# The S5 layer's input matrices in a hybrid diffusion step: computed by broadcast products in the layout they are stored in, instead of by TensorE transposes

## The chip, the cores and the metric

One core of one Trainium2 chip runs the whole program once. The metric is the device time of one execution in microseconds. Three runs of the kernel before took 3233.06, 3233.39 and 3234.0 us; their median, 3233.39 us, is the time before.

## What is computed

The reference is one inference step of a four-layer backbone on 640 tokens (512 latent, 128 context) of width 1024: attention, an S5 layer, attention, attention, each followed by a gated convolutional FFN of width 2816. Only layer 1, the S5 layer, concerns this change. It has 64 groups of 16 channels, and each group has a 64-dimensional complex diagonal state per direction:

```python
a_re, a_im, bb_re, bb_im = s5_discretize(lam_re, lam_im, log_dt, b_re, b_im)
br = jnp.einsum('bsgc,gpc->bsgp', ug, bb_re)
bi = jnp.einsum('bsgc,gpc->bsgp', ug, bb_im)
hr, hi = complex_scan(a_re, a_im, br, bi, reverse)
y_dir = jnp.einsum('bsgp,gcp->bsgc', hr, c_re) - jnp.einsum('bsgp,gcp->bsgc', hi, c_im)
```

The kernel does not scan token by token. It takes eight tokens at a time: for a chunk, the state gains the sum over the eight tokens of a^k * B * u, with k from 7 down to 0 (0 up to 7 in the backward direction). The matrix of a^k * B for one group, with token and channel (8 x 16 = 128) on the rows and the state (64) on the columns, once for the real and once for the imaginary part, is the group's **input matrix**, W. It depends on weights alone.

## The kernel before, in words

All activations are float32 and each dense product is three float32r matmuls (high x high, high x low, low x high; `mm3`, L295 to L299). A weight tile takes this way (`weights`, L317): its load goes into a `raw` tile (pool of 3, L266), ScalarE rounds it to `wh` (L302), VectorE takes the rest as `wl` (L306); `wh` and `wl` have 2 buffers each. TensorE reads `wh` and `wl`, and the `raw` tile is free again when both parts are made.

The order: layer 0's attention, its output projection (`project_out`, L1068), layer 0's FFN (`ffn`, L688, from about 365 to 895 us in the trace), then layer 1, the S5 layer (`s5`, L1348), and so on. Work for the S5 layer that needs only weights is put beside the layer before it, as a list of small pieces, `todo`, from which `side(n)` (L679) takes n pieces at fixed points. The tile framework then orders each engine's instructions by the order of the text and by when it reckons them ready, allots pool buffers, and places the waits; every engine and the SP queue, which issues nearly all DMAs, work strictly in that written order.

**Parameters** (`s5_params`, L1119) run beside layer 0's output projection, in seven pieces. VectorE computes a and the factor of B for 64 rows x 128 (`four`, L1160), TensorE transposes them (L1181), VectorE forms the powers a^0 to a^8 (`pw`, L1183 to L1193, by `cmul`, L1103, all with one scratch tile `tmp`), GpSimd copies the powers into `par` in two orders, 36 copies for the output matrices (L1206) and 32 for the input matrices (L1211), VectorE forms B (`bb`, L1237), and one DMA writes `par` to DRAM as `d_par` (L1241). The initial state is loaded and transposed last (L1244 to L1251).

**Matrices** (`s5_matrices`, L1253) run in FFN 0: 16 steps (8 blocks of 4 state pairs x 2 directions), each of four pieces, mixed with 8 pieces that load a modulation weight into a `raw` tile (L1728). `up(m)` (L736) calls `side` twice, mostly for two pieces. In a step, the first piece loads `s5par` from `d_par` (L1265), forms the output matrices P on VectorE (real) and GpSimd (imaginary), three products of 128x576 on each (L1278 to L1280), and stores them (L1283); ScalarE fills `bz` (L1292). The second does 8 small matmuls for the lags (L1299). The third copies those out (L1305 to L1312) and forms Q, the input matrices with the state on the partitions, three operations of 128x512 on each of VectorE and GpSimd (L1320 to L1322), into the buffer that P had. The fourth has TensorE transpose Q in 8 pieces of 128x128 (L1328), ScalarE copy the result out of PSUM into W in `scr` by four copies of 128x256 (L1331), and SP store W to `d_w1` (L1334). P and Q share one buffer per part, `s5par` has one buffer, and W is one place in `scr`.

Of the kernel before, what the change touches and what calls it, by code (L numbers as in the profile page):

```python
# [252 lines left out]
class Kernel:  # L253
# [865 lines left out]
    def s5_params(self, sp):  # L1119
# [4 lines left out]
        self.d_par = self.dram.tile([16, 128, 392], F32, name="d_par")  # L1124
# [64 lines left out]
        tmp = sp.tile([128, 1024], F32, name="tmp")  # L1189
        for lo in (1, 2, 4):  # L1190
# [6 lines left out]
        par = sp.tile([128, 16, 392], F32, name="par")  # L1197
        for d in range(2):
            blks = slice(8 * d, 8 * d + 8)
            xs = slice(32 * d, 32 * d + 32)  # L1200
            for r in range(2):
                for q in range(9):
                    k = q if d == 0 else 8 - q
                    src = pw[:, k, r, xs].rearrange("p (b g) -> p b g", g=4)
                    o = r * 36 + q * 4
                    nc.gpsimd.tensor_copy(out=par[:, blks, o:o + 4], in_=src)  # L1206
                for q in range(8):
                    k = 7 - q if d == 0 else q
                    src = pw[:, k, r, xs].rearrange("p (b g) -> p b g", g=4)
                    o = 72 + r * 32 + q * 4  # L1210
                    nc.gpsimd.tensor_copy(out=par[:, blks, o:o + 4], in_=src)  # L1211
        yield

        for r, n in enumerate(("re", "im")):
# [3 lines left out]
            for b4 in range(4):  # L1218
# [4 lines left out]
                for t in range(2):  # L1223
                    pv = p[0:64, :].rearrange("p (b g t c) -> p t b g c", b=4, g=4, t=2)[:, t]
                    self.copy(par[t * 64:(t + 1) * 64, 4 * b4:4 * b4 + 4, 136 + r * 64:200 + r * 64]
                              .rearrange("p b (g c) -> p b g c", c=16), pv)
            yield

# [9 lines left out]
        for r in range(2):  # L1238
            nc.gpsimd.tensor_copy(out=par[:, :, 264 + r * 64:328 + r * 64],
                                  in_=bb[:, r].rearrange("p (b g) c -> p b (g c)", g=4))  # L1240
        nc.sync.dma_start(out=self.d_par.rearrange("b p x -> p b x"), in_=par)  # L1241
        yield

        st = self.raw()  # L1244
        nc.sync.dma_start(out=st[:, 0:128], in_=i["state_l1"][0].rearrange("d r (g t) p -> (d r g) (t p)", t=2))
        p = self.bankB()
        nc.tensor.transpose(out=p[:, 0:128], in_=st[:, 0:128], identity=self.ident)
        self.s0 = self.const.tile([128, 2, 2, 32], F32, name="s0")
        for r in range(2):
            v.tensor_scalar(out=self.s0[:, r], in0=p[:, 0:128].rearrange("p (d r g) -> p r d g", d=2, r=2)[:, r],  # L1250
                            scalar1=-1.0 if r else 1.0, scalar2=None, op0=ALU.mult)  # L1251

    def s5_matrices(self, pool):  # L1253

        nc = self.nc
        st = {}

        def step(blk, d):
            if (blk, d) == (0, 0):
# [4 lines left out]
            pr = pool.tile([128, 392], F32, tag="s5par", name="s5par")  # L1264
# [3 lines left out]
            w1p = [pr[:, 72 + r * 32:104 + r * 32].rearrange("p (q g) -> p g q", g=4).unsqueeze(3)  # L1268
                   .to_broadcast([128, 4, 8, 16]) for r in range(2)]
            ct = [pr[:, 136 + r * 64:200 + r * 64].rearrange("p (g c) -> p g c", c=16) for r in range(2)]  # L1270
            bb = [pr[:, 264 + r * 64:328 + r * 64].rearrange("p (g c) -> p g c", c=16) for r in range(2)]
# [41 lines left out]

            W = scr[:, 0:1024].rearrange("p (q n) -> p q n", q=8)
# [8 lines left out]
            yield  # L1323
            for h in range(2):
                p = self.bankB()
                for g in range(2):
                    for r in range(2):
# [468 lines left out]
```

## Time and profile before

| | |
|---|---|
| median of three runs | 3233.39 us |
| the profiled execution: its own time | 3232.56 us |
| its span, first to last instruction | 3230.7 us |
| mean granted TensorE clock, as a share of full speed | 0.986 |
| busy share: TensorE / weight load / VectorE / ScalarE / GpSimd | 97% / 91% / 67% / 44% / 17% |
| DMA moved | 364.30 MB, mean 113 GB/s |
| chain that ended last, by engine | TensorE 79%, VectorE 12%, ScalarE 4%, DMA 3% |

How to read it: the own time holds some 1.9 us around the span. Busy shares are means over very different stages; TensorE's busy time counts a matmul from start to modelled end, and matmuls overlap, so what one costs is read from the distance between starts. The chain is followed back from the last instruction to what released it. Line numbers are those of the code above; L302 and L306 are helpers, told apart by their tiles. "issue" as a releaser is time in which the engine waited for nothing that the profile shows.

### The profile page before, as it was taken

What the parts mean: (1) busy time and instruction counts of PE and PEld (TensorE: products, weight loads), DVE (VectorE), ACT (ScalarE), POOL (GpSimd) and SP (SyncE); (2) the same over time, 40 slices, a digit from 0 to 9 for tenths busy, and PEclk for the clock granted to TensorE, in tenths of its full rate; (3) what the DMA queues carried; (4) which work ended last, traced back from release to release, by engine and by line L of the source; (5) the groups of instructions that cost most, each with busy time, mean ns of one, the idle gap of its engine ahead of it and who ended that gap; (6) DMA issues with size and microseconds to landing.
All of it is one profiled execution on the core that took longest, in us unless ns stands there. A gap on an engine that the chain in (4) does not pass through costs nothing.

```text
span 3230.7 us, 55544 instructions
## 1 busy us (share of the span) xinstructions
PE 3120.2 (97%) x22620; PEld 2933.3 (91%) x22620; DVE 2157.9 (67%) x4070; ACT 1410.7 (44%) x2497; POOL 534.1 (17%) x916
## 2 busy tenths in 40 slices
PE   7999999989978999999999999999999999999999
PEld 6867999989966999999999889999998878999999
DVE  6666886797677368867766658677656775644543
ACT  4466443343442343433443655343344574533432
POOL 1332332353210000000013520000001431000000
PEclk8999999999998999999999999999999999999999
DMA  6251554444465324544431023344424212223221
GB/s 247 88 191 49 143 169 142 126 118 111 147 257 186 107 72 139 155 118 131 131 115 60 27 72 87 116 121 120 115 84 152 73 40 73 64 82 87 63 86 46
DMA packets 384287, 364.30 MB, mean 113 GB/s; under 512 B 39144, under 2 KB 357488, under 8 KB 374432
## 3 DMA queue, kind: packets, MB, share of 16 engines
q1 hardware_dynamic: 382752, 356.55, 35.5%
q0 software_dynamic: 1280, 4.20, 0.4%
q8 instruction: 178, 2.92, 0.4%
q14 instruction: 77, 0.63, 0.1%
HBM read 328.07 MB, written 36.83 MB: 113 GB/s over the span
## 4 chain that ended last, share of the span: by engine, by line
PE 79%; DVE 12%; ACT 4%; DMA 3%; issue 2%; POOL 1%; SPq 0%; DVEq 0%; ACTq 0%; POOLq 0%
PE psa L297 16%; PE psa L299 16%; PE psa L298 16%; PE psb L297 6%; PE psb L299 6%; PE psb L298 6%; PE psb L176 3%; PE psb L206 2%; DVE wl L306 2%; PE psb L440 1%; PE psa L110 1%; PE psa L111 1%; ACT wh L302 1%; DVE Pt L1470 1%; DVE t L715 1%
## 5 line engine op out<-in xcount | busy, mean ns | idle before, releaser
L297 PE MATMUL psa<-yh,wh 128*128 128x384 f32 (+1 forms) x2752 | 854.3, 310 | 2.6 <-ACT hb L705 1.8
L299 PE MATMUL psa<-yh,wl 128*128 128x384 f32 (+1 forms) x2752 | 850.0, 309 | 0.0
L298 PE MATMUL psa<-yl,wh 128*128 128x384 f32 (+1 forms) x2752 | 849.7, 309 | 0.3 <-POOL yl L232 0.3
L306 DVE TENSOR_TENSOR wl<-raw,wh 128x2048 fp32r<-128x2048 f32 (+2 forms) x192 | 408.9, 2130 | 269.8 <-ACT wh L302 266.1
L297 PEld LDWEIGHTS psa<-yh,wh 128*128 128x128 f32 x2752 | 521.6, 190 | 18.8 <-issue 10.3
L302 ACT ACTIVATE wh<-raw 128x2048 fp32r<-128x2048 f32 (+2 forms) x192 | 333.1, 1735 | 465.9 <-PE psa L298 428.8
L298 PEld LDWEIGHTS psa<-yl,wh 128*128 128x128 f32 x2752 | 522.1, 190 | 0.5 <-POOL yl L232 0.5
L299 PEld LDWEIGHTS psa<-yh,wl 128*128 128x128 f32 x2752 | 521.7, 190 | 0.0
L297 PE MATMUL psa<-ah,wh 128*128 128x384 f32 (+1 forms) x1184 | 366.7, 310 | 7.3 <-DVE X L663 7.3
L299 PE MATMUL psa<-ah,wl 128*128 128x384 f32 (+1 forms) x1184 | 365.7, 309 | 0.0
L298 PE MATMUL psa<-al,wh 128*128 128x384 f32 (+1 forms) x1184 | 365.5, 309 | 0.0
L663 DVE SCALAR_TENSOR_TENSOR X<-psa,modt,X 128x256 f32<-128x256 f32 x372 | 141.5, 433 | 218.7 <-PE psa L299 218.7
L306 POOL TENSOR_TENSOR yl<-scr,yh 128x256 fp32r<-128x256 f32 (+1 forms) x36 | 41.3, 1150 | 1273.5 <-ACT yh L302 1247.5
L297 PEld LDWEIGHTS psa<-ah,wh 128*128 128x128 f32 x1184 | 224.2, 189 | 12.7 <-issue 7.3
L297 PE MATMUL psb<-wh,yh 128*128 128x256 f32 x800 | 227.7, 286 | 2.6 <-ACT yh L602 2.5
L299 PE MATMUL psb<-wh,yl 128*128 128x256 f32 x800 | 226.4, 286 | 3.9 <-DVE yl L603 1.9
L298 PE MATMUL psb<-wl,yh 128*128 128x256 f32 x800 | 226.2, 285 | 0.3 <-DVE wl L306 0.3
L298 PEld LDWEIGHTS psa<-al,wh 128*128 128x128 f32 x1184 | 224.3, 189 | 0.0
L299 PEld LDWEIGHTS psa<-ah,wl 128*128 128x128 f32 x1184 | 224.1, 189 | 0.0
L497 DVE SCALAR_TENSOR_TENSOR acc<-raw,cond,acc 128x512 f32<-128x512 f32 x280 | 197.1, 745 | 33.2 <-DMA raw<-in_w_mod_dram 33.2
L715 DVE SCALAR_TENSOR_TENSOR t<-hb,cols,t 128x641 f32<-128x641 f32 x176 | 170.5, 970 | 57.6 <-ACT t L713 57.6
L705 ACT ACTIVATE hb<-psa,cols 128x512 f32<-128x512 f32 x320 | 149.9, 519 | 124.3 <-PE psa L299 124.2
(327 smaller groups left out, 6253.0 us busy)
## 6 DMA issues: line engine op xcount, KB each, us to landing
raw<-in_w_up_dram SPq DMA_DIRECT2D x176, 512.0 KB, 5.2
raw<-in_w_mod_dram SPq DMA_DIRECT2D x80, 512.0 KB, 3.9
raw<-in_w_mod_dram SPq DMA_DIRECT2D x35, 1024.0 KB, 5.1
raw<-in_w_down_dram SPq DMA_DIRECT2D x48, 640.0 KB, 3.9
raw<-in_l_w_qkv_dram SPq DMA_DIRECT2D x20, 1024.0 KB, 5.8
raw<-d_w SPq DMA_DIRECT2D x16, 1024.0 KB, 6.4
raw<-in_w_down_dram SPq DMA_DIRECT2D x16, 896.0 KB, 4.6
raw<-in_l_w_o_dram SPq DMA_DIRECT2D x12, 1024.0 KB, 5.1
```

The lines of the kernel that those rows point to most:

```text
L110: mm(out=out, lhsT=qt, rhs=kh, start=True, stop=False)
L176: nc.tensor.transpose(out=pt[:, o:o + 128], in_=self.Ps[g][:, c:c + 128], identity=K.ident)
L206: mm(out=po[64 * par:64 * par + 64, 0:256], lhsT=self.at.vraw[:, self.keys[i][b], self.kv * 64:self.kv * 64 + 64], rhs=PT[:, par], start=b ...
L297: mm(out=out, lhsT=wh, rhs=xh, start=start, stop=False)
L298: mm(out=out, lhsT=wh, rhs=xl, start=False, stop=False)
L299: mm(out=out, lhsT=wl, rhs=xh, start=False, stop=stop)
L302: self.nc.scalar.activation(out=out, in_=in_, func=ACTF.Copy)
L306: (sub or self.nc.vector).tensor_tensor(out=l, in0=x, in1=h.bitcast(F32), op=ALU.subtract)
L497: nc.vector.scalar_tensor_tensor(out=a, in0=st["w"][:, s], scalar=w, in1=a, op0=ALU.mult, op1=ALU.add)
L663: self.nc.vector.scalar_tensor_tensor(out=self.X[:, d, s0:s1], in0=p[:, o:o + s1 - s0], scalar=m[:, v, gate + d:gate + d + 1], in1=self.X[ ...
L705: nc.scalar.activation(out=hb[:, s0 + o - (s0 // 512) * 512:s1 + o - (s0 // 512) * 512], in_=p[:, b + s0:b + s1], func=ACTF.Identity, bias ...
L715: nc.vector.scalar_tensor_tensor(out=t, in0=hb[:, 0:641], scalar=kc[0], in1=t, op0=ALU.mult, op1=ALU.add)
```

## The change

Input matrices are no longer formed as Q and transposed. They are formed in the layout of W at once: partition = (token q, channel c), columns = (group, state). For that, the powers have to stand on all 16 partitions of a token and B on the 8 x 16 partitions of every token, and DMAs with repeated source rows bring them there.

In the parameters: VectorE forms powers 0 to 7 once more, in the layout before the transpose (`pq`, 64 partitions, 18 operations of 128, 256 and 384 columns), and nine DMAs store them as `d_pq`. After `bb`, 16 transposes turn B, four ScalarE copies of 128x512 negate it into a `raw` tile, and eight DMAs store it as `d_bc`. The 32 GpSimd copies of L1211 go, `par` and `d_par` shrink from 392 to 328 columns. The piece for the initial state comes ahead of the B piece instead of behind it.

In each of the 16 steps: the third piece takes a `raw` tile and issues four DMAs of 256 KB (real and imaginary powers, real and imaginary B); the fourth forms W by three operations of 128x512 on VectorE (real half) and three on GpSimd (imaginary half), and stores it. The 8 transposes and the 4 ScalarE copies go.

```diff
+        pq = sp.tile([64, 8, 2, 128], F32, name="pq")
...
+        for lo, n in ((1, 1), (2, 2), (4, 3)):
+            bc = lambda r: pq[:, lo, r].unsqueeze(1).to_broadcast([64, n, 128])
+            self.cmul(v, pq[:, lo + 1:lo + n + 1, 0], pq[:, lo + 1:lo + n + 1, 1], pq[:, 1:n + 1, 0],
+                      pq[:, 1:n + 1, 1], bc(0), bc(1), tmp[0:64, 0:n * 128].rearrange("p (k x) -> p k x", k=n))
+        for k in range(8):
+            nc.sync.dma_start(out=self.d_pq[0, 7 - k].rearrange("r x n -> x r n"), in_=pq[0:32, k])
+        nc.sync.dma_start(out=self.d_pq[1].rearrange("q r x n -> x (q r) n"),
+                          in_=pq[32:64].rearrange("x q r n -> x (q r) n"))
...
-                for q in range(8):
-                    k = 7 - q if d == 0 else q
-                    src = pw[:, k, r, xs].rearrange("p (b g) -> p b g", g=4)
-                    o = 72 + r * 32 + q * 4
-                    nc.gpsimd.tensor_copy(out=par[:, blks, o:o + 4], in_=src)
...
+        bt = self.raw().rearrange("p (r b n) -> p r b n", r=2, b=8)
+        for r in range(2):
+            for h in range(2):
+                p = self.bankB()
+                for b in range(4):
+                    nc.tensor.transpose(out=p[:, b * 128:(b + 1) * 128],
+                                        in_=bb[:, r, 8 * (4 * h + b):8 * (4 * h + b + 1)].rearrange("p x c -> p (x c)"),
+                                        identity=self.ident)
+                nc.scalar.activation(out=bt[:, r, 4 * h:4 * h + 4], in_=p.rearrange("p (b n) -> p b n", b=4),
+                                     func=ACTF.Identity, scale=-1.0)
+        for x in range(8):
+            nc.sync.dma_start(out=self.d_bc[:, :, x // 4, :, x % 4].rearrange("r b c n -> c (r b) n"),
+                              in_=bt[16 * x:16 * x + 16].rearrange("c r b n -> c (r b) n"))
         nc.sync.dma_start(out=self.d_par.rearrange("b p x -> p b x"), in_=par)
...
+            raw = self.raw()
+            pq, nb = (raw[:, 1024 * k:1024 * k + 1024].rearrange("p (r n) -> p r n", r=2) for k in range(2))
+
+            for r in range(2):
+                nc.sync.dma_start(out=pq[:, r], in_=self.d_pq[d, :, r, 4 * blk:4 * blk + 4].rearrange("q g n -> q (g n)")
+                                  .unsqueeze(1).to_broadcast([8, 16, 512]))
+                nc.sync.dma_start(out=nb[:, r], in_=self.d_bc[r, 4 * d + blk // 2, blk % 2].rearrange("c g n -> c (g n)")
+                                  .unsqueeze(0).to_broadcast([8, 16, 512]))
+            yield
             W = scr[:, 0:1024].rearrange("p (q n) -> p q n", q=8)
-            b4 = [b.unsqueeze(2).to_broadcast([128, 4, 8, 16]) for b in bb]
-            Q = [pool.tile([128, 4, 8, 16], F32, tag="s5P%d" % r, name="s5Q") for r in range(2)]
+            Wr = [W[:, :, 64 * r:64 * r + 64] for r in range(2)]
+            g8 = lambda z: z.rearrange("p (g n) -> p g n", g=8)
             for r, eng in enumerate((nc.vector, nc.gpsimd)):
                 tt = eng.tensor_tensor
-                tm = t[r][:, :, 0:8]
-                tt(out=Q[r], in0=b4[0], in1=w1p[r], op=ALU.mult)
-                tt(out=tm, in0=b4[1], in1=w1p[1 - r], op=ALU.mult)
-                tt(out=Q[r], in0=Q[r], in1=tm, op=ALU.subtract if r == 0 else ALU.add)
-            yield
-            for h in range(2):
...
-                        nc.tensor.transpose(out=p[:, (r * 2 + g) * 128:(r * 2 + g + 1) * 128],
-                                            in_=Q[r][:, 2 * h + g].rearrange("p q c -> p (q c)"), identity=self.ident)
-                for r in range(2):
-                    nc.scalar.activation(out=W[:, 4 * h:4 * h + 4, r * 64:(r + 1) * 64],
-                                         in_=p[:, r * 256:(r + 1) * 256].rearrange("p (g n) -> p g n", n=64),
-                                         func=ACTF.Identity, scale=-1.0 if r else 1.0)
+                tm = g8(scr[:, 1024 + 576 * r:1536 + 576 * r])
+                tt(out=Wr[r], in0=g8(nb[:, 1 - r]), in1=g8(pq[:, 1]), op=ALU.mult)
+                tt(out=tm, in0=g8(nb[:, r]), in1=g8(pq[:, 0]), op=ALU.mult)
+                tt(out=Wr[r], in0=Wr[r], in1=tm, op=ALU.add if r else ALU.subtract)
             nc.sync.dma_start(out=self.d_w1[blk].rearrange("q (g d n) -> q g d n", d=2, n=128)[:, :, d], in_=W)
```

## Rows read from the trace of the kernel before

**Rows 1.** the page, busy time, share of the span and instructions of each engine.
```profile
PE 3120.2 (97%) x22620; PEld 2933.3 (91%) x22620; DVE 2157.9 (67%) x4070; ACT 1410.7 (44%) x2497; POOL 534.1 (17%) x916
```

**Rows 2.** windows view: us, busy PE, PEld, DVE, ACT, POOL (instructions), PEclk, DMA share, GB/s.
```profile
418.00:436.00 18.00, 18.00 (x142) 16.74 (x139) 13.64 (x14) 9.62 (x17) 6.70 (x7) 1.00 0.59 176
...
640.00:658.00 18.00, 18.00 (x141) 17.43 (x140) 17.04 (x14) 7.70 (x19) 11.30 (x8) 1.00 0.37 107
658.00:676.00 18.00, 15.70 (x111) 14.93 (x110) 17.13 (x17) 8.72 (x19) 11.55 (x8) 0.93 0.39 114
770.00:790.00 20.00, 20.00 (x160) 18.97 (x159) 19.12 (x18) 8.85 (x18) 13.34 (x8) 1.00 0.53 145
```

**Rows 3.** timeline of PE around one step's transposes: start, duration, instruction.
```profile
638.10 0.34 PE L299 MATMUL psa<-yh,wl 128*128 128x384 f32 x1
638.27 1.04 PE L1328 MATMUL psb<-ident,s5Q 128*128 128x128 f32 x8
639.06 0.36 PE L297 MATMUL psa<-yh,wh 128*128 128x256 f32 x1
639.26 0.28 PE L298 MATMUL psa<-yl,wh 128*128 128x256 f32 x1
639.38 0.28 PE L299 MATMUL psa<-yh,wl 128*128 128x256 f32 x1
```

**Rows 4.** the line view of L1328, TensorE: duration ns min/median/max, first and last start.
```profile
L1328 PE MATMUL psb<-ident,s5Q x128: 270/273/329, 425.3 to 836.1; 128*128 128x128 f32 x128
```

**Rows 5.** waits of PE, 395 to 905 us: total us, times, longest.
```profile
PE psb L1328 <- DVE s5Q L1322: 4.8, 3, 2.3
```

**Rows 6.** the line view of L1331, ScalarE.
```profile
L1331 ACT ACTIVATE scr<-psb x64: 379/393/412, 429.3 to 841.2; 128x256 f32<-128x256 f32 x64
```

**Rows 7.** the line view of L1320, VectorE.
```profile
L1320 DVE TENSOR_TENSOR s5Q<-s5par x16: 679/688/1790, 413.8 to 827.9; 128x512 f32<-128x512 f32 x16
```

**Rows 8.** waits of the SP queue, 400 to 905 us: total us, times, longest.
```profile
SPq L329 <- DVE wl L306: 74.4, 12, 9.7
SPq L457 <- DVE wl L306: 38.8, 8, 8.2
SPq L331 <- DVE wl L306: 28.5, 9, 8.0
```

**Rows 9.** the view of DMA issues: count, KB each, median us to landing.
```profile
raw<-in_w_mod_dram SPq DMA_DIRECT2D x35, 1024.0 KB, 5.1
...
wl<-in_w_mod_dram SPq DMA_DIRECT2D x7, 1024.0 KB, 12.2
...
s5par<-d_par SPq DMA_DIRECT2D x16, 196.0 KB, 2.3
```

**Rows 10.** the tile view of s5par: its load, and who waited for it (us, times).
```profile
L1265 SPq DMA_DIRECT2D s5par<-d_par x16: 332/336/424, 363.7 to 797.9; - x16
...
  ACT s5bz L1292: 40.2, 15
```

**Rows 11.** timeline of DVE, 318 to 345 us, in brackets the idle time before.
```profile
319.68 0.42 DVE L540 TENSOR_TENSOR scr<-scr 128x256 f32<-128x256 f32 x1 [0.41 <-ACT scr L539]
321.54 0.29 DVE L1187 COPY pw<-psb 128x128 f32<-128x128 f32 x1 [1.44 <-PE psb L1181]
...
322.55 0.56 DVE L540 TENSOR_TENSOR scr<-scr 128x384 f32<-128x384 f32 x1
...
329.05 1.23 DVE L1107 TENSOR_TENSOR bb<-raw,ff 128x1024 f32<-128x1024 f32 x1 [2.56 <-DMA raw<-in_l_b_re_dram]
...
341.55 2.29 DVE L306 TENSOR_TENSOR wl<-raw,wh 128x2048 fp32r<-128x2048 f32 x1
```

**Rows 12.** timeline of PE, 340 to 345 us.
```profile
343.90 0.39 PE L299 MATMUL psb<-yh,wl 128*128 128x256 f32 x1 [0.81 <-DVE wl L306]
```

**Rows 13.** timeline of ACT, 355 to 376 us.
```profile
369.00 1.05 ACT L1292 ACTIVATE s5bz<-s5par 64x64 f32<-64x64 f32 x4 [7.21 <-DMA s5par<-d_par]
```

**Rows 14.** the line view of L1211, GpSimd.
```profile
L1211 POOL COPY par<-pw x32: 205/212/2271, 306.8 to 346.8; 128x32 f32<-128x32 f32 x32
```

More of the change, by code (lines that the diff above doesn't have):

```diff
@@ L1123, in s5_params @@
         M, A_, S_ = ALU.mult, ALU.add, ALU.subtract
-        self.d_par = self.dram.tile([16, 128, 392], F32, name="d_par")
+        self.d_par = self.dram.tile([16, 128, 328], F32, name="d_par")
+        self.d_pq = self.dram.tile([2, 8, 2, 32, 128], F32, name="d_pq")
+        self.d_bc = self.dram.tile([2, 8, 2, 16, 4, 128], F32, name="d_bc")
         self.d_a8 = self.dram.tile([128, 2, 64], F32, name="d_a8")
@@ L1189, in s5_params @@
         tmp = sp.tile([128, 1024], F32, name="tmp")
+        pq = sp.tile([64, 8, 2, 128], F32, name="pq")
+        nc.vector.memset(pq[:, 0, 0], 1.0)
+        nc.vector.memset(pq[:, 0, 1], 0.0)
+        v.tensor_copy(out=pq[:, 1], in_=four[:, 0:2])
+        for lo, n in ((1, 1), (2, 2), (4, 3)):
[6 more added lines that the diff above has]
+                          in_=pq[32:64].rearrange("x q r n -> x (q r) n"))
         for lo in (1, 2, 4):
@@ L1195, in s5_params @@
         yield
-        par = sp.tile([128, 16, 392], F32, name="par")
+        par = sp.tile([128, 16, 328], F32, name="par")
         for d in range(2):
@@ L1224, in s5_params @@
                     pv = p[0:64, :].rearrange("p (b g t c) -> p t b g c", b=4, g=4, t=2)[:, t]
-                    self.copy(par[t * 64:(t + 1) * 64, 4 * b4:4 * b4 + 4, 136 + r * 64:200 + r * 64]
+                    self.copy(par[t * 64:(t + 1) * 64, 4 * b4:4 * b4 + 4, 72 + r * 64:136 + r * 64]
                               .rearrange("p b (g c) -> p b g c", c=16), pv)
             yield
+        st = self.raw()
+        nc.sync.dma_start(out=st[:, 0:128], in_=i["state_l1"][0].rearrange("d r (g t) p -> (d r g) (t p)", t=2))
+        p = self.bankB()
+        nc.tensor.transpose(out=p[:, 0:128], in_=st[:, 0:128], identity=self.ident)
+        self.s0 = self.const.tile([128, 2, 2, 32], F32, name="s0")
+        for r in range(2):
+            v.tensor_scalar(out=self.s0[:, r], in0=p[:, 0:128].rearrange("p (d r g) -> p r d g", d=2, r=2)[:, r],
+                            scalar1=-1.0 if r else 1.0, scalar2=None, op0=ALU.mult)
+        yield
         bs = []
@@ L1263, in step @@
             scr = st["scr"]
-            pr = pool.tile([128, 392], F32, tag="s5par", name="s5par")
+            pr = pool.tile([128, 328], F32, tag="s5par", name="s5par")
             nc.sync.dma_start(out=pr, in_=self.d_par[8 * d + blk])
@@ L1267, in step @@
                    .to_broadcast([128, 4, 9, 16]) for r in range(2)]
[L1268 to L1271, printed above, removed]
+            ct = [pr[:, 72 + r * 64:136 + r * 64].rearrange("p (g c) -> p g c", c=16) for r in range(2)]
+            bb = [pr[:, 200 + r * 64:264 + r * 64].rearrange("p (g c) -> p g c", c=16) for r in range(2)]
             P = [pool.tile([128, 4, 9, 16], F32, tag="s5P%d" % r, name="s5P") for r in range(2)]
```

17 lines of the change are left out of this document (4 added, 13 removed).

## The prediction

> **What bounds the kernel now.** I read the page's first part first: TensorE is busy for 97% of the span, no other engine for more than 67% [rows 1]. So a gain has to come off TensorE's own queue or off a wait that TensorE has. The input matrices are built in FFN 0, so I next cut that stage into windows of about one loop over `up`, some 18 us. There the reader is to see two kinds of loop. In the first TensorE is busy for all of the loop and VectorE for 13.6 of 18 us: TensorE sets the pace. In the second VectorE is busy for 17.0 to 19.1 us of 18 to 20, and in one of them TensorE has 2.3 us of gaps and the granted clock is 0.93 [rows 2]: there VectorE sets the pace or nearly does, and time taken off TensorE alone turns into a wait. Then I looked for what the changed lines cost TensorE. In the timeline a step's eight transposes start 0.79 us before the next dense matmul, and that matmul is followed 0.20 us later where the one after it is followed 0.12 us later: 0.87 us per step [rows 3], with 128 transposes in all [rows 4]. The waits of TensorE in this stage add that it stood before them three times for 4.8 us in total, because VectorE's Q was late [rows 5]. Last I read what the SP queue waits for: 29 weight loads stood there for 74.4 + 38.8 + 28.5 = 141.7 us until VectorE had emptied a `raw` tile [rows 8]. The pool of three is always full, and the change asks for one more tile per step.
>
> **The change, part by part.**
>
> Transposes in the loops: 16 steps x 0.87 us [rows 3] = 13.9 us off TensorE. Where TensorE sets the pace all of it counts.
>
> The wait for Q: TensorE no longer waits for the S5 step's VectorE work here, at most 4.8 us [rows 5]. These three waits lie in loops where VectorE is full, so part comes back at the next thing TensorE needs of VectorE, the split of the next weights (L306). Bounds 0 and 4.8; I take half, 2.4.
>
> ScalarE: 64 copies x 0.39 us = 25 us go [rows 6], but ScalarE is busy for under 10 us of each 18 [rows 2]; nothing on the path.
>
> VectorE and GpSimd: three operations of 128x512 on each before and after, 0.69 us on VectorE [rows 7]. Nothing, while the data are there when they are reached.
>
> The four transfers of a step: 1 MB in all. SP spends 0.34 us on an issue [rows 10], 4 x 0.34 = 1.3 us per step, covered by the time it stands waiting for `raw` tiles; without that cover the next weight load is 1.3 us later, and its split has most of a loop to spare. Their landing is not shown by any row. Nearest rows: 196 KB of `s5par` land in 2.3 us, one 1 MB load into `raw` in 5.1 us, and beside heavy traffic in 12.2 us [rows 9]. I take 5.1, the row nearest in size and place. What hides it: a `raw` tile is taken as soon as one falls free, in program order, so the transfers can run a step ahead like the modulation loads. Bounds for what VectorE waits: 0 below, 12.2 - 5.1 = 7.1 us per step above. I take 0, and the first rival takes the rest.
>
> The extra `raw` tile: a loop needs one weight tile and in the early loops one modulation tile, each held some 5 us for landing [rows 9] and 5 us to be emptied; with S held for 5.1 us and then three operations, that is some 30 us of 3 x 18 = 54 tile-microseconds. Nothing; if the order is unlucky, a load waits for a tile and shows first as a late L306.
>
> Dependencies that fall: P and Q no longer share a buffer, and `s5par` is read for P and `bz` only. The next step may start earlier. Below nothing; I take nothing.
>
> Parameters: 18 operations on VectorE at 0.29, 0.42 and 0.56 us for 128, 256 and 384 columns [rows 11], 6 x 1.27 = 7.6 us, ahead of `pw` and `bb`, which share `tmp` with them. Gaps of 0.41, 1.44 and 2.56 us there can take up 4.4; 3.2 us are left. The split of the output projection's weights comes behind that chain, and TensorE already waits 0.81 us for it [rows 11, 12], so these 3.2 us fall on TensorE. Sixteen transposes cost 16 x 0.87 / 8 = 1.7 us there. Four ScalarE copies lie in idle time. Eight issues for `d_bc` stand on SP ahead of `d_par`, 8 x 0.34 = 2.7 us, and what follows `d_par`, the first load of `s5par`, already holds ScalarE for 7.21 us in front of the FFN's normalised input [rows 13]. Against it 32 GpSimd copies x 0.21 = 6.8 us go ahead of `d_par` [rows 14]; GpSimd has to wait for the later `bb` anyway, so I count 0.9 us of it. Nine issues for `d_pq` stand on SP ahead of a weight load, whose cover is the wait for `raw`. Sum 3.2 + 2.7 - 0.9 = +5.0, bounds 0 (the gaps take all of VectorE's part, GpSimd's 6.8 us cover SP's) and 10.3 (all 7.6 and all 2.7).
>
> Sum: -13.9 - 2.4 + 1.7 + 5.0 = -9.6 us. The profiled execution took 3232.56 us, its span 3230.7 and 1.9 around it; that gives 3223.0. The median of the runs is 0.83 us above the profiled one, so I say 3223.8.
>
> **The rivals.**
>
> *The matrices arrive late (slower).* In 10 of the 16 steps both pieces, transfers and products, are taken by one `side` call, so in the written order the products may stand right behind their data. VectorE works in order: if the data are late, the convolutions and the weight splits behind the products wait too, and TensorE with them where VectorE is full. For it: ScalarE stood 15 times for 40.2 us before `s5par`, 2.7 us each, though that load lands in 2.3 [rows 9, 10], and VectorE 2.56 us before B [rows 11]; the order seems written for faster loads. Price: 10 x 2.7 = 27 us, 3232.6 - 9.6 + 27 = 3250.0. It decides from 1 us of waiting per step (no gain) and 1.6 us (0.2% slower). Against it: `raw` tiles are filled as far ahead as there are tiles. With landing twice as long as the 1 MB row, 10.2 us, the wait would be 2.7 + 5.1 = 7.8 us and the time 3232.6 - 9.6 + 78 = 3301. The Trainium skill, "DMA: Bandwidth & Descriptors", section "Rules for kernel authors", speaks for just that: it says that an outermost dimension below 16, such as a leading broadcast, confines a DMA to that many engines, and all four transfers have 8 outermost. By that rule half of the 16 engines carry them and the landing is the doubled one; no row here shows such a transfer, so it adds to this rival's chance. 0.20.
>
> *No change.* Where VectorE is full the loops keep their length, half of the 13.9 us turns into waits for splits, the 2.4 us come back too, and the parameters cost what I say: -7.0 + 1.7 + 5.0 = -0.3, 3232.3. For it: VectorE's 17 us of 18 [rows 2] don't shrink. Against: gaps are in few loops. 0.22.
>
> *More than forecast.* TensorE, no longer tied to Q, runs ahead of VectorE through the full loops, which catch up in the `down` phases where VectorE has room. All 4.8 us stay gained, the 2.3 us gaps as in [rows 2] go in about two and a half more loops (6 us), the clock returns (0.07 of 18 us, 1.3), and the parameters cost nothing beyond TensorE's 1.7: -13.9 - 4.8 - 6 - 1.3 + 1.7 = -24.3, 3208.3, or 3209 on the median's scale. Against: the convolutions VectorE falls behind with feed the next `down`. 0.13.
>
> That the change doesn't do what it says is no rival: transposes and copies go from the code.
>
> **How the numbers follow.** The forecast has 0.45. Median runs tell 0.2%, 6.5 us, from no change. Faster by more: the forecast but for its upper edge, 0.42, and the third rival, 0.13: 0.55. Within 0.2%: 0.03 of the forecast and the second rival: 0.25. Slower: the first, 0.20. The range runs from 3209, the third rival's time, up to 3244, which is the first rival at 2.0 us per step; left out are the rest of that rival, 0.13, and what lies under the third, 0.05.
>
> **What would show it.** Right: no transposes in FFN 0, TensorE's busy time in full loops unchanged and the loops 0.87 us shorter, the span from 300 to 375 us some 5 us longer. VectorE's products with idle time of under 1 us before them, released by something else than the DMA. Wrong: "DMA raw" as the releaser of over 1.6 us per step before VectorE's first product; transfers landing after 10 us; L306 of the weights waiting for its `raw` tile; or the stage before the FFN longer by over 10.3 us.

## The result, and the profile after

The change made the kernel slower: 3280.5 us (3279.4 to 3282.8) against 3233.7 for the kernel before on the same chip, a ratio of 1.0144, 95% interval 1.0132 to 1.0156. That is +46.8 us where -9.6 was forecast. The profiled execution of after took 3282.8 us, its span 3280.6.

The page's first part of after, which answers to [rows 1]: TensorE is busy as long as before, although the loops' 128 transposes are gone, and the span is 50 us longer.

```profile
PE 3122.9 (95%) x22508; PEld 2935.1 (89%) x22508; DVE 2155.8 (66%) x4091; ACT 1397.2 (43%) x2437; POOL 516.3 (16%) x884
```

The place of the loss shows in two line views of after, the first load of the S5 stage (894.7 us before) and the loads of X, of which the last started at 2694.0 us before. The first load of X starts when it did (300.2), the S5 stage 51.4 us later, and nothing is added after it (50.9). So the loss lies between 300 and 946 us: the parameters and FFN 0.

```profile
L1400 SPq DMA_DIRECT2D a<-d_a x1: 327/327/327, 946.1 to 946.1; - x1
L1076 SPq DMA_DIRECT2D X<-d_x x12: 338/424/677, 300.2 to 2744.9; - x12
```

After runs behind before by 18 to 28 us here, so equal times hold different work. The windows compared go, in whole microseconds, from one store of W to the next, for the same three steps (columns as in [rows 2]). First before:

```profile
662.00:680.00 18.00, 15.70 (x112) 15.15 (x112) 17.12 (x17) 8.72 (x19) 11.55 (x8) 0.91 0.39 114
680.00:699.00 19.00, 17.87 (x132) 16.81 (x131) 17.46 (x16) 8.45 (x19) 12.23 (x8) 1.00 0.35 102
699.00:717.00 18.00, 16.14 (x124) 15.62 (x125) 16.41 (x17) 8.20 (x18) 10.82 (x8) 1.00 0.39 114
```

Then after:

```profile
680.00:701.00 21.00, 14.35 (x100) 13.58 (x99) 15.61 (x15) 6.94 (x14) 9.39 (x7) 0.84 0.58 162
701.00:725.00 24.00, 17.48 (x119) 16.71 (x119) 16.45 (x17) 9.23 (x16) 9.40 (x7) 0.86 0.48 129
725.00:745.00 20.00, 15.74 (x107) 14.97 (x106) 15.26 (x14) 6.36 (x14) 9.45 (x7) 0.91 0.50 145
```

The three steps take 65 us instead of 55. VectorE, which stood still for 4.0 us in all, now does so for 17.7, TensorE's gaps grow from 5.3 to 17.4 us, and the granted clock is 0.84 to 0.91 instead of 0.91 to 1.00.

The waits of VectorE, ScalarE and TensorE of after, 395 to 905 us (us in total, times, longest), say what VectorE stands for.

```profile
DVE scr L1352 <- DMA raw<-d_bc: 37.6, 12, 6.3
...
DVE scr L1353 <- DMA raw<-d_bc: 19.5, 7, 3.2
DVE scr L1352 <- issue: 14.0, 3, 7.0
```
```profile
ACT t L722 <- DVE t L717: 83.4, 21, 12.2
```
```profile
PE psa L297 <- ACT hb L705: 31.8, 8, 7.3
PE psa L297 <- DVE X L663: 8.3, 5, 3.2
```

Read as a chain: VectorE's products (L1352, L1353) wait 57.1 us for the four transfers. Another 14.0 us before L1352 have no releaser in the profile; they are probably the same wait, since e3 below, with faster transfers, has none of them. The convolution (L717) stands behind them in VectorE's queue, ScalarE's gate (L722) waits for it (83.4 us; 23.7 in the same stretch before), the next evacuation (L705) stands behind that in ScalarE's queue, and TensorE waits for its bank: 31.8 us, where the kernel before had 1.8.

One step, in the timelines of SP and VectorE of after (start, duration, in brackets the idle time before):

```profile
643.49 0.59 SPq L1341 DMA_DIRECT2D raw<-d_pq  x1
...
645.36 0.57 SPq L1343 DMA_DIRECT2D raw<-d_bc  x1
```
```profile
649.07 0.69 DVE L1353 TENSOR_TENSOR scr<-raw 128x512 f32<-128x512 f32 x1 [2.74 <-DMA raw<-d_bc]
652.03 0.69 DVE L1352 TENSOR_TENSOR scr<-raw 128x512 f32<-128x512 f32 x1 [2.27 <-DMA raw<-d_bc]
```

VectorE goes on 6.7 us after the issue of the last transfer and 8.5 us after that of the first. The windows of those microseconds, one by one (the last two columns are DMA share and GB/s), point to why: with nothing else running, the four transfers of 256 KB keep half of the DMA engines busy.

```profile
647.00:648.00 1.00, 1.00 (x8) 1.00 (x7) 0.00 (x0) 0.00 (x0) 0.00 (x0) 1.00 0.52 199
648.00:649.00 1.00, 1.00 (x8) 1.00 (x7) 0.00 (x0) 0.00 (x0) 0.00 (x0) 1.00 0.52 168
...
650.00:651.00 1.00, 1.00 (x11) 1.00 (x11) 0.00 (x0) 1.00 (x1) 0.19 (x1) 1.00 0.51 199
651.00:652.00 1.00, 1.00 (x9) 1.00 (x8) 0.00 (x0) 0.29 (x1) 1.00 (x1) 1.00 0.10 37
```

The Trainium skill, "DMA: Bandwidth & Descriptors", section "Rules for kernel authors", states that an outermost dimension below 16 confines a transfer to at most that many engines. Eight are outermost here, and the share of 0.52 agrees.

Ahead of the FFN the waits of TensorE of after, 318 to 430 us, hold one that the kernel before does not have: before B's transposes.

```profile
PE psb L1268 <- DVE bb L1109: 10.1, 1, 10.1
PE psb L297 <- ACT wh L302: 2.4, 1, 2.4
```

Behind that pause the granted clock is lower. In the windows of after it is 0.72 from 330 to 360 us and 0.50, half of full speed, from 350 to 355 us; in the kernel before it is 1.00 from 330 to 360 us.

```profile
330.00:360.00 30.00, 18.65 (x116) 17.99 (x115) 20.16 (x37) 6.64 (x11) 11.11 (x35) 0.72 0.82 172
350.00:355.00 5.00, 5.00 (x26) 5.00 (x25) 0.00 (x0) 1.19 (x2) 0.51 (x1) 0.50 0.72 258
```

Over the whole profiled execution it is 0.977 instead of 0.986. The nine groups of dense matmuls in the fifth part of the page, equal in number, are busy for 16.4 us more in sum (they overlap, so the time lost is less). So part of what the waits cost is probably clock; no run separates it.

SP's timeline of after: the second half of B, loaded at 323.63 before, comes at 334.90, and the eight stores of B occupy the queue for 10.8 us ahead of weight loads.

```profile
334.90 0.42 SPq L1254 DMA_DIRECT2D raw<-in_l_b_im_dram  x1
...
352.15 10.80 SPq L1274 DMA_DIRECT2D d_bc<-raw  x8
363.06 1.75 SPq L329 DMA_DIRECT2D raw<-in_w_up_dram  x2
```

But the load is not what TensorE waits for. In VectorE's timeline of after B's first product (L1107) starts at 341.55 us with no idle time before it; the split of the output projection's weights and the norm stand ahead of it. Before, it started at 329.05, ahead of that split [rows 11].

```profile
338.07 2.29 DVE L306 TENSOR_TENSOR wl<-raw,wh 128x2048 fp32r<-128x2048 f32 x1 [0.57 <-ACT wh L302]
340.28 1.35 DVE L540 TENSOR_TENSOR scr<-scr 128x384 f32<-128x384 f32 x3
341.55 1.22 DVE L1107 TENSOR_TENSOR bb<-raw,ff 128x1024 f32<-128x1024 f32 x1
```

### The profile page after: what moved, and what is told of

It reads as the page before. It is cut to its first block, busy times and chain, and to the rows that moved or that the text cites. A ratio compares the mean times of both kernels' runs of the same rounds, so it can differ in the third digit from the quotient of the medians.

```text
span 3280.6 us, 55405 instructions
## 1 busy us (share of the span) xinstructions
PE 3122.9 (95%) x22508; PEld 2935.1 (89%) x22508; DVE 2155.8 (66%) x4091; ACT 1397.2 (43%) x2437; POOL 516.3 (16%) x884
## 4 chain that ended last, share of the span: by engine, by line
PE 78%; DVE 10%; DMA 4%; ACT 3%; issue 2%; POOL 1%; SPq 1%; DVEq 0%; POOLq 0%; ACTq 0%
PE psa L297 16%; PE psa L299 16%; PE psa L298 16%; PE psb L297 6%; PE psb L299 6%; PE psb L298 6%; PE psb L176 3%; DMA raw<-d_bc 2%; PE psb L206 2%; DVE wl L306 2%; PE psa L110 1%; PE psb L440 1%; ACT wh L302 1%; PE psa L111 1%; DVE Pt L1491 1%
## 5 line engine op out<-in xcount | busy, mean ns | idle before, releaser
L306 DVE TENSOR_TENSOR wl<-raw,wh 128x2048 fp32r<-128x2048 f32 (+2 forms) x192 | 408.9, 2130 | 277.8 <-ACT wh L302 276.7
L297 PEld LDWEIGHTS psa<-yh,wh 128*128 128x128 f32 x2752 | 526.5, 191 | 49.8 <-ACT hb L705 34.7
L306 POOL TENSOR_TENSOR yl<-scr,yh 128x256 fp32r<-128x256 f32 (+1 forms) x36 | 41.5, 1155 | 1274.3 <-ACT yh L302 1248.3
L497 DVE SCALAR_TENSOR_TENSOR acc<-raw,cond,acc 128x512 f32<-128x512 f32 x280 | 197.3, 746 | 31.8 <-DMA raw<-in_w_mod_dram 31.5
L705 ACT ACTIVATE hb<-psa,cols 128x512 f32<-128x512 f32 x320 | 150.3, 519 | 128.6 <-PE psa L299 128.5
L715 DVE SCALAR_TENSOR_TENSOR t<-hb,cols,t 128x641 f32<-128x641 f32 x176 | 162.5, 925 | 60.0 <-ACT t L713 60.0
## 6 DMA issues: line engine op xcount, KB each, us to landing
raw<-in_w_down_dram SPq DMA_DIRECT2D x16, 896.0 KB
```

The costliest lines, as they stand in the source:

```text
L297: mm(out=out, lhsT=wh, rhs=xh, start=start, stop=False)
L306: (sub or self.nc.vector).tensor_tensor(out=l, in0=x, in1=h.bitcast(F32), op=ALU.subtract)
L497: nc.vector.scalar_tensor_tensor(out=a, in0=st["w"][:, s], scalar=w, in1=a, op0=ALU.mult, op1=ALU.add)
L705: nc.scalar.activation(out=hb[:, s0 + o - (s0 // 512) * 512:s1 + o - (s0 // 512) * 512], in_=p[:, b + s0:b + s1], func=ACTF.Identity, bias ...
L715: nc.vector.scalar_tensor_tensor(out=t, in0=hb[:, 0:641], scalar=kc[0], in1=t, op0=ALU.mult, op1=ALU.add)
```

## The experiments

Times are medians; the kernel before gave 3233.3 to 3234.7 us beside each group. Theory at the start: late transfers make the loss in the loops (the first rival of the prediction), the start-up a smaller part. Rival: the new order on VectorE makes it, whatever the data do.

**One half each.** e1 has the new parameters with the old loops; e2 the new loops with the old parameters, reading rows of `w_mod` of the same shapes.

```
- in_=self.d_pq[d, :, r, 4 * blk:4 * blk + 4].rearrange("q g n -> q (g n)")
+ in_=self.i["w_mod"][d, 8 * r:8 * r + 8, 512 * blk:512 * blk + 512]
```

> The new parameter work alone (pq, d_pq, the transposes of B, d_bc, the state piece moved); the 16 steps are those of the kernel before, with its 32 GpSimd copies, and d_pq and d_bc are read by nobody. Theory (the loss has two parts, one of them ahead of FFN 0): in the changed kernel the FFN's first evacuation comes 8.1 us later and the first lag matmuls 19.2 us later, so 3242 to 3253 us, and TensorE waits some 10 us for B's transposes around 345 us. Rival (what is lost ahead of the FFN is made up in it, the loops alone are slow): at most 3238 us.

> The new steps alone, with the parameters of the kernel before: the four transfers read rows of the modulation weights in access patterns of the same shape (8 outermost), so the values are not the input matrices. Theory (the transfers land after 8 to 9 us on half of the DMA engines and VectorE stands behind them): 3262 to 3272 us, VectorE idle for some 60 us before its products with the transfer as the releaser, DMA share near 0.5 while only these transfers run. Rival (the loops are only slow because their start is late and d_par and d_bc crowd the queue): at most 3225 us, the 13.9 us of transposes gained.

e1: 3249.0 us, +15.3 (1.0050, 1.0035 to 1.0065). e2: 3268.2, +34.5 (1.0106, 1.0091 to 1.0121). Together 49.8 against 46.8: the halves add, within the scatter.

**The channels outermost**, so that 16 instead of 8 lead every transfer; rows of W are permuted back when it is stored, in longer runs (nothing in FFN 0 waits for that store, here or in after).

```
- .unsqueeze(1).to_broadcast([8, 16, 512]))
+ .unsqueeze(0).to_broadcast([16, 8, 512]))
- nc.sync.dma_start(out=self.d_w1[blk].rearrange("q (g d n) -> q g d n", d=2, n=128)[:, :, d], in_=W)
+ nc.sync.dma_start(out=self.d_w1[blk].rearrange("(q c) (d x) -> c q d x", c=16, d=2)[:, :, d],
+                   in_=scr[:, 0:1024])
```

> The changed kernel with the channel outermost (16) and the token inside (8) in the four transfers; the partitions of W change places and its store puts the rows back, with the directions apart so that a store writes 4 KB runs. Theory (8 outermost confines a transfer to 8 engines): DMA share near 1 while they run, landing after 5 to 6 us instead of 8.5, VectorE's waits halved, 3255 to 3268 us. Rival (the engines don't matter, the re-read rows or the issue set the landing): share stays near 0.5, landing over 8 us, 3276 us or more.

3259.0 us, 21.5 below after. VectorE's waits of e3, 430 to 890 us, fall from 57.1 to 36.7 us in all; its view of DMA issues gives a landing of 4.5 and 4.7 us a transfer, and its windows show a DMA share of 1.00 while they run. So the eight-engine form costs 21.5 us, the lost clock included.

```profile
DVE scr L1352 <- DMA raw<-d_bc: 16.8, 11, 3.4
...
DVE scr L1353 <- DMA raw<-d_bc: 10.5, 7, 2.4
DVE scr L1352 <- DMA raw<-d_pq: 9.4, 2, 5.0
```
```profile
raw<-d_pq SPq DMA_DIRECT2D x32, 256.0 KB, 4.5
raw<-d_bc SPq DMA_DIRECT2D x32, 256.0 KB, 4.7
```
```profile
651.00:652.00 1.00, 1.00 (x9) 1.00 (x8) 0.00 (x0) 0.00 (x0) 0.00 (x0) 1.00 1.00 223
```

**No transfers at all**: the products read constant columns.

```
- raw = self.raw()
- pq, nb = (raw[:, 1024 * k:1024 * k + 1024].rearrange("p (r n) -> p r n", r=2) for k in range(2))
+ pq, nb = (self.cols[:, 512 * k:512 * k + 512].unsqueeze(1).to_broadcast([128, 2, 512]) for k in range(2))
```

> The changed kernel without the four transfers and without the raw tile: the products read a constant tile (cols), so W holds other values. Parameters, d_pq and d_bc as changed. Theory (the transfers' lateness is the loss of the loops, and without it the transposes' 13.9 us are gained): 3228 to 3240 us, of which 8 to 19 us are the parameters' cost. Rival (the loops are slow because VectorE's and GpSimd's products now collide or are ordered badly, not for want of data): 3255 us or more.

3273.0 us: the theory missed. With nothing to wait for, the tile framework wrote the first product right behind the previous step's store of W, and there VectorE waited for that store. In VectorE's timeline of e4 the weight split (L306) follows that wait:

```profile
670.71 1.68 DVE L1302 TENSOR_TENSOR scr<-s5par 128x576 f32<-128x576 f32 x1
674.83 0.69 DVE L1345 TENSOR_TENSOR scr<-cols 128x512 f32<-128x512 f32 x1 [2.44 <-DMA d_w<-scr]
675.44 3.38 DVE L306 TENSOR_TENSOR wl<-raw,wh 128x2048 fp32r<-128x2048 f32 x1
```

In the kernel before ScalarE wrote W; now VectorE writes its real half in place. e5 and e6 give W's real half two places in turn; e5 thereby also stores W in runs of 4 KB instead of 512 bytes.

```
- Wr = [W[:, :, 64 * r:64 * r + 64] for r in range(2)]
+ Wr = [g8(scr[:, o:o + 512]) for o in (1024 * d, 512)]
```

> This is e4_no_transfers (no transfers, VectorE and GpSimd multiply constant columns, so W holds other values) with one thing more: W's real half, which VectorE writes, lies in two places of scr in turn, so that a step's products don't wait for the store of the step before; the imaginary half stays single. Theory, that the store of W held VectorE in e4 (3273.0 us, in which the parameters are 15.3 by e1): without that wait the loops win what was forecast for them, up to 16.3, or at least lose nothing: 3233 to 3252 us, and the wait of VectorE's first product for the DMA of W (26.9 us in e4) is gone from the list of waits. Rival, that e4 was slow for another reason (the products stand ahead of the weight splits and the convolutions in VectorE's queue, whatever they wait for, or the clock): 3264 us or more.

> This is e3_channel_outer (real transfers with the 16 channels outermost) with W's real half in two places in turn. Theory, that e3's remaining loss in the loops (3259.0 against 3249.0 with the new parameters alone, 10.0 us, against a forecast gain of up to 16.3) is partly the wait for W's store: 3245 to 3255 us. Rival, that in e3 the landing of the transfers ends last anyway, so that the store is done by then: within 2.5 us of e3, 3256.5 to 3261.5 us, with the waits for the transfers (36.7 us in all on VectorE) as they were.

e5: 3262.6 us, 10.4 below e4, but VectorE still shows this wait (16.6 us instead of 26.9), though the columns no longer overlap; why was not found. The store itself lands in 3.1 us instead of 3.8 (medians), so the shorter wait is no proof that the second place helped. e5 falls between both expectations, and what the rest of e4's loss is, the place of the products or something else, stays open. e6: 3256.6, 2.4 below e3, inside the scatter of either, as its rival said: with real transfers no engine waits for the store of W in FFN 0, in after and e3 as well.

**The transfers a piece earlier**, on e6:

```
             yield
+            raw = self.raw()
+            pq, nb = (raw[:, 1024 * k:1024 * k + 1024].rearrange("p (r n) -> p r n", r=2) for k in range(2))
...
             p = self.bankB()
             l0 = d
```

> This is e6_room_channel with the four transfers issued one piece earlier, before the lag matmuls' piece instead of after it, so that one more dense part of some 9 us lies between issue and first product. Theory, that what is left of the loops' loss is the landing time: VectorE's waits for the transfers fall from some 37 us to under 8, and the time is 5 to 15 us under e6's. Rival, that SyncE reaches the transfers no earlier because it waits for raw tiles, or that a raw tile held a part longer delays the weight loads by as much: within 2.5 us of e6's time, or above it, and SyncE's waits for raw tiles grow.

3248.8 us, 7.8 below e6, as expected in size, but not by the mechanism expected: VectorE's waits for the transfers fall only from 37.8 to 35.2 us, not under 8. TensorE's waits from 395 to 905 us fall from 31.6 to 24.9 us in all; why, no run shows. The new loops now cost what the old ones do (e1: 3249.0); the forecast gain of 16.3 us is missing.

**All products on GpSimd**, so that VectorE need not wait for transfers:

```
- for r, eng in enumerate((nc.vector, nc.gpsimd)):
-     tt = eng.tensor_tensor
+ for r in range(2):
+     tt = nc.gpsimd.tensor_tensor
```

> This is e8_early with all six products of the input matrix on GpSimd, so that VectorE, which stands ahead of the weight splits and the convolutions, never waits for a transfer. Theory, that what still keeps the loops from their forecast gain is VectorE standing still for the transfers in the middle of its convolutions (35.2 us of such waits in e8 between 430 and 890 us): those waits are gone, and the time is 6 to 16 us under e8, 3233 to 3243 us. Rival, that GpSimd, at some 1.75 us a product, gets the bound of a step (twelve operations, about 21 us, against 18 us for a step) and TensorE waits for its part of P: 3249 us or more.

3289.8 us: the rival, so e12 does not show what the loops are worth without these waits. In the waits of e12 VectorE stands for GpSimd and for `s5par` instead.

```profile
DVE scr L1302 <- DMA s5par<-d_par: 40.3, 5, 9.4
DVE scr L1302 <- POOL scr L1353: 38.4, 9, 6.7
```

**The gain by itself**: the kernel before, its eight transposes per step taken out.

```
-                p = self.bankB()
-                for g in range(2):
...
-                                         in_=p[:, r * 256:(r + 1) * 256].rearrange("p (g n) -> p g n", n=64),
+                                         in_=Q[r][:, 2 * h:2 * h + 2].rearrange("p g q c -> p (g q c)")
+                                         .rearrange("p (g n) -> p g n", n=64),
```

> This is the kernel before without the eight transposes of a step: ScalarE copies the products Q into W straight from their tiles (W's columns are then those of Q untransposed), all else as it was. It measures the one term that was to carry the gain. Theory, that TensorE bounds the loops and the transposes take 0.87 us a step of it: 3233.7 less 13.9, with the 2.4 us of waits for Q up to 16.3, so 3217 to 3222 us. Rival, that the order in which VectorE and ScalarE deliver (weight splits, convolutions) bounds the loops as much, so that TensorE only waits elsewhere: 3226 to 3236 us.

3230.7 us, 3.4 less; ratio 0.9990, 0.9981 to 1.0000. The rival. In its profiled execution, with 3234.9 us the slowest of its ten, FFN 0 ends no earlier (S5's first load at 896.0 us, 894.7 before), and TensorE, freed of the transposes, waits for ScalarE's evacuations: 10.6 us, 1.8 before. Waits of TensorE of e15, 400 to 895 us:

```profile
PE psa L297 <- ACT hb L705: 10.6, 7, 2.7
PE psa L297 <- DVE X L663: 8.8, 4, 3.9
```

e15 is not quite the gain alone: it keeps ScalarE's 64 copies, which the change does not have, and they now wait 10.3 us for Q in ScalarE's queue, among the gates and evacuations. What the relief gives without them was not tried.

**The start-up, by moving.** e7 lets ScalarE issue the 17 stores; e9 puts the loads of B first again; e10 is e9 with the stores of B issued by GpSimd; e11 is e8 with e10's parameters.

```
-            nc.sync.dma_start(out=self.d_bc[:, :, x // 4, :, x % 4].rearrange("r b c n -> c (r b) n"),
+            nc.scalar.dma_start(out=self.d_bc[:, :, x // 4, :, x % 4].rearrange("r b c n -> c (r b) n"),
```

> This is e1_params_only (new parameters, old loops) with the 17 stores of the powers and of B issued by ScalarE instead of SyncE. Theory, that e1's 15.3 us come from SyncE's order (the stores of the powers hold the load of B's imaginary half from 323.6 to 332.7 us, the eight stores of B hold the first FFN weights from 349.5 to 364.8): 3235 to 3241 us. Rival, that they come from the work itself (about twenty products on VectorE, sixteen transposes on TensorE in front of its dense matmuls): 3246 to 3252 us.

> This is e1_params_only (new parameters, old loops, 3249.0 us) with two parts moved in the text: the powers pq with their nine stores stand behind the store of par, and the initial state is last again, as in the kernel before, so that the loads of B stand ahead of both on SyncE. Theory, that TensorE's 10.2 us wait for B's product in e1 (before the sixteen transposes) comes from B's imaginary half being loaded at 332.7 instead of 323.6 us: the wait falls under 3 us and the time to 3238 to 3245 us. Rival, that the wait only moves on to the FFN's first tiles, because the stores of B (1.54 us each on their queue, 12.3 us for eight) still stand ahead of the first weights: 3246 to 3252 us.

> This is e9_loads_first with the eight stores of B issued by GpSimd instead of SyncE, so that they don't stand ahead of the first FFN weights (ScalarE as issuer, in e7, put them ahead of its part of the norm and gave 3255.9 us). Theory, that the 12.3 us that these stores take on a queue are the rest of the parameters' cost: 3 to 8 us under e9, 3232 to 3240 us. Rival, that the first weights wait for raw tiles and the norm at that time anyway, or that GpSimd's other work ahead of the FFN comes late: within 2 us of e9 or above it.

> This is e8_early (the whole change with the channels outermost, W's real half twofold, the transfers a piece earlier; 3248.8 us) with the parameters as in e10_pool_stores. Theory, that loops and start-up add: 3248.8 less what e10 wins against e1 (3249.0), so about equal to e10, within 4 us of it, and faster than the kernel before if e10 is under 3234. Rival, that a part of what is won at the start is taken back in the loops (they begin earlier, and no later wait goes): 5 us or more above e10.

e7: 3255.9, 6.9 above e1, outside both expectations: ScalarE spent 12.3 us issuing the stores of B, and its next part of the norm (L539) had to stand behind them. e9: 3247.8, the rival: B's first product starts at 329.28 us again, ahead of the weight split, and TensorE's wait for B fell from 10.2 to 2.5 us, but it waits 7.5 us for the first FFN weights, which now stand on SP behind all the stores. Waits of TensorE of e9, 318 to 430 us, and its window 360 to 390 us, where the DMA share is 1.01:

```profile
PE psb L297 <- ACT wh L302: 7.5, 1, 7.5
PE psb L299 <- DVE wl L306: 2.9, 2, 1.8
PE psb L1248 <- DVE bb L1109: 2.5, 1, 2.5
```
```profile
360.00:390.00 30.00, 21.43 (x113) 20.65 (x113) 16.96 (x34) 9.93 (x15) 0.78 (x13) 0.77 1.01 263
```

e10: 3253.4, above e9, as the rival said: TensorE's wait for the first FFN weights grew from 7.5 to 9.3 us, and the DMA engines stayed nearly full (share 0.95 from 360 to 370 us). e11: 3247.8, 1.0 under e8, not faster than the kernel before, and 5.6 under e10, so the sum that was expected (within 4 us of e10) missed.

e13 stores B in 4 KB runs by two DMAs.

```
-        for x in range(8):
-            nc.sync.dma_start(out=self.d_bc[:, :, x // 4, :, x % 4].rearrange("r b c n -> c (r b) n"),
-                              in_=bt[16 * x:16 * x + 16].rearrange("c r b n -> c (r b) n"))
+            nc.sync.dma_start(out=self.d_bc[r].rearrange("c b h x n -> (c b) (h x) n"), in_=bt[:, r])
```

> This is e1_params_only (new parameters, old loops, 3249.0 us) with the loads of B and the initial state as in the kernel before, the nine stores of the powers behind the loads of B, and B held as (rows, channel, block), so that its transposes are stored by two DMAs of 4 KB runs instead of eight of 512-byte runs. Theory, from e9 and e10: the cost of the parameters is 1.5 MB of stores in 512-byte runs, which fill the DMA engines (share 1.01 from 360 to 390 us in e9) just ahead of the first FFN weights, and the late load of B; with both mended 3235 to 3242 us. Rival, that the sixteen transposes, four evacuations and some twenty products in that stretch cost it by their own time: 3245 us or more.

3266.4 us, inconclusive: my edit also put the state's load behind `par`'s store, and TensorE waited 21.8 us for it. e14, e13's parameters with e8's loops, had the same fault (3264.6).

**The start-up, by taking away.** e16, e17 and e18 are e1 without the stores of B, of the powers, and of both.

```
-        for x in range(8):
-            nc.sync.dma_start(out=self.d_bc[:, :, x // 4, :, x % 4].rearrange("r b c n -> c (r b) n"),
-                              in_=bt[16 * x:16 * x + 16].rearrange("c r b n -> c (r b) n"))
```

> This is e1_params_only (new parameters, old loops that read neither new tensor; 3249.0 us) without the eight stores of B, which is left out (transposes and evacuations stay). Theory, that the stores' 12.7 us on SyncE ahead of the first FFN weights are one of two equal causes of e1's 15.3 us, the late load of B behind the stores of the powers the other: 5 to 10 us less, 3239 to 3244 us, with the 10.2 us wait for B's product still there. Rival, that the first weights wait for the norm or raw tiles anyhow: 3247 us or more.

> This is e1_params_only without the nine stores of the powers (their products stay). Theory of two equal causes: the load of B's imaginary half comes earlier, TensorE's wait for B's product falls from 10.2 us to under 4, and the time to 3239 to 3244 us. Rival, from e9 (there the wait had fallen to 2.5 us and the time only by 1.2): 3246 to 3250 us, because what TensorE doesn't wait here it waits at the first weights, behind the stores of B.

> This is e1_params_only without either set of stores, seventeen left out. Theory, that the stores on SyncE make the parameters' cost: 3234 to 3239 us, so that sixteen transposes, four evacuations and some twenty products together cost at most the 5 us that I forecast for the parameters. Rival, that this work itself makes the cost in its stretch: 3244 us or more.

e16: 3244.6 (-4.4), just between its two expectations. e17: 3247.3 (-1.7), the rival's time. e18: 3241.7 (-7.3), between its two and still 1.0027 (1.0015 to 1.0039) of the kernel before. So of the 15.3 us the stores are 7.3, and 8.0 are the work and its order. All three keep one wait of TensorE, 318 to 430 us; in e18:

```profile
PE psb L1266 <- DVE bb L1109: 10.2, 1, 10.2
```

In e17 and e18 B's second half is loaded at 330.8 and 330.4 us, with no store of the powers ahead of it; SP's waits of e18 have its issue stand 7.2 us for a `raw` tile, which a weight split frees (`SPq L1252 <- DVE wl L306`). In after it came at 334.9. TensorE's wait is 10.1 or 10.2 us in all of them, and in e18's timeline B's first product again has no idle time before it and stands behind the split:

```profile
337.14 2.35 DVE L306 TENSOR_TENSOR wl<-raw,wh 128x2048 fp32r<-128x2048 f32 x1 [0.48 <-ACT wh L302]
339.42 1.38 DVE L540 TENSOR_TENSOR scr<-scr 128x384 f32<-128x384 f32 x3
340.72 1.22 DVE L1107 TENSOR_TENSOR bb<-raw,ff 128x1024 f32<-128x1024 f32 x1
```

My account in e7's expectation, that the stores make the wait by holding back the load, falls. What makes it is the place of B's products in VectorE's written order. Of the two parts that e9 moved back, the state's load and the powers, which one changed that order was not tried.

## Why the prediction was wrong

The step that cost most is this one: "Bounds for what VectorE waits: 0 below, 12.2 - 5.1 = 7.1 us per step above. I take 0". The runs show 57.1 us of such waits, 3.6 us per step, inside the bounds and far from 0. Of the time, 21.5 us come back when the landing is shortened (e3) and 7.8 when the transfers are issued earlier (e8). The choice of 5.1 us failed with it: that row is a load of 128 rows, the four transfers kept half of the engines busy, and VectorE went on 8.5 us after the first issue. "The transfers can run a step ahead" failed too: in the waits of SP of after, 400 to 905 us, the transfers' own issue stands for a `raw` tile that VectorE empties, and the products come a few microseconds behind it.

```profile
SPq L1341 <- DVE wl L306: 41.7, 11, 8.3
```

The sign does not hang on this step alone: e8, with 35.2 us of the waits left, is still 14.7 us slower than the kernel before, and the two terms below failed as well.

The first rival was right in its mechanism (products right behind their data, everything behind them in VectorE's queue late, TensorE last) and had a chance of 0.20. That its price, 27 us, is near the 29.3 is partly luck: the waits of VectorE were twice as long, and the time that came back is about half of them. Its time of 3250 was too low because the forecast's gain and its 5.0 us for the parameters were built into it.

The term "16 steps x 0.87 us" = 13.9 us off TensorE, with 2.4 us for Q, was to give 16.3 us; e15, with the reservation above, gives 3.4. TensorE was freed, but then waited for ScalarE and VectorE. The prediction itself had loops where "VectorE sets the pace or nearly does", and the second rival had that step at 0.22; I counted the 13.9 us in full all the same.

The parameters' term, +5.0 us with bounds 0 and 10.3, measured +15.3. Two parts of it were wrong. Stores were priced at an SP issue of 0.34 us; a store of B took 10.8 / 8 = 1.35 on average, and all stores together 7.3 us of time (e18). And the sixteen transposes were priced at their own 1.7 us, not at what they wait for. The prediction let the weight split come behind B's products, as in [rows 11]; in the written order of after the split stands ahead of them, B comes 12.5 us later than before, and TensorE, whose dense matmuls stand behind the transposes, stops for 10.1 us and then runs at half clock for a while.

The term for the dependencies that fall ("Below nothing; I take nothing") came out as nothing, but not for its reason: there is a new dependency, on the store of W, which holds VectorE in e4. In the change itself no engine waits for that store in FFN 0.

Right was the sign to look for, "DMA raw" as releaser of over 1.6 us per step. The terms set at nothing for SP's issues (0.58 us each instead of 0.34) and ScalarE's copies were not tried by themselves.

The account of the loss is then: parameters 15.3 (e1), eight-engine transfers 21.5 (e3), late issue 7.8 (e8), and 2.4 within the scatter (e6). That this adds up to 47.0 of 46.8 is no check of its own: the last three are the way from after to e8, and e8 happens to equal e1. It leaves nothing for the gain. Whether that is because TensorE's relief is worth little here, as e15 suggests, or because the 35.2 us of waits left in e8 eat it, the runs do not separate. No version of the change beat the kernel before; the nearest whole one is e11. What would be won by B loaded first with its stores after the first weights was not tried.

## What to carry to other kernels

Before pricing work taken off the busiest engine, look at the engine beside it in the same windows: where that one is as full, the work may be worth far less than its time (here, in e15, 3.4 of 16.3 us). When an operation starts to read a transfer instead of computing from data at hand, what counts is what stands behind it in its engine's queue, so price the landing in the transfer's own shape (here 8 rows outermost took half of the engines) and issue it a piece earlier. A transpose or a store put ahead of other work costs what it waits for or what the queue holds, not its own duration. When two kernels have drifted apart, compare windows of the same work, not of the same times.

## What the runs showed that I had not expected

Issue time on a queue varies: 0.34 us for `s5par` [rows 10], 0.58 for a 256 KB broadcast, and 0.46 to 2.10, 1.35 on average, for the eight 128 KB stores of B from 16 partitions in 512-byte runs. GpSimd issued the same eight stores in 4.7 us (e10), and then seven stores of the powers on SP took 17.3 us instead of the 3.9 of e9. In e13 the two stores of B in 4 KB runs took 0.33 us each.

The order that the framework writes can matter as much as the data: with the transfers gone, e4 was slower than e3 with them, and in after B's products were written behind a weight split although nothing on VectorE waited for B's load.
